# Attention loads in halves on a fixed SyncE order, turns in pairs, later memory rows and more gate matmuls in the memory attention's tail

## The chip, the cores and the metric

The kernel runs on one core of a Trainium2 chip. The metric is the device time of one execution in microseconds (us). The kernel before was timed in three runs: median 2069.23 us, from 2068.04 to 2072.08. One more execution was profiled; all rows of the profile and of the trace come from it.

## What is computed

The reference is a decoder trunk of two layers in float32 on x of 1024 tokens x 1024. Layer 0 mixes by dilated causal window attention in three groups of 8 heads, whose outputs are merged per head by their softmax denominators. Layer 1 mixes by a gated linear recurrence (HGRN2). Each layer also attends with 4 heads to 256 memory tokens and multiplies by a gate.

```python
for l in range(DEPTH):
    h = rms_norm(x, norm_gain[l])
    if l % 2 == 0:
        cols = h @ w_in_a[j]
        mix = dilated_mixer(cols[..., :3 * A_QKV], cos, sin, q_gain_a[j], k_gain_a[j])
        q_mem = cols[..., 3 * A_QKV:3 * A_QKV + MEM_WIDTH]
        gate = cols[..., 3 * A_QKV + MEM_WIDTH:]
...
    mem_out = memory_cross_attention(q_mem, mem, mem_norm_gain[l], w_mem_kv[l],
                                     mem_q_gain[l], mem_k_gain[l])
    y = jnp.concatenate([mix, mem_out], axis=-1) * jax.nn.silu(gate)
    x = x + y @ w_out
...
def dilated_mixer(cols, cos, sin, q_gain, k_gain):
...
    for g, (window, dil) in enumerate(DIL_PAIRS):
        o, lse = dilated_window_attention(q[:, :, g], k[:, :, g], v[:, :, g], dil, window // dil)
...
    alpha = jax.nn.softmax(jnp.stack(lses, axis=0), axis=0)
    o = jnp.sum(alpha[..., None] * jnp.stack(outs, axis=0), axis=0)
```

The groups are (128, 1), (512, 4) and (2048, 16): window and dilation. Head dimension is 128.

## The kernel before

**Engines and names.** TensorE (PE) multiplies and turns (transposes). ScalarE (ACT), VectorE (DVE) and GpSimd (POOL) work beside it, and SyncE (SP) issues nearly all DMAs, in the order of one queue: an issue that must wait holds back all that stand behind it. A product is made of three matmuls on a high and a low part of each side (wh, wl; hi, lo), which accumulate in a PSUM bank: tiles `acc` (three of them), `s` (two), `pt` (two, for turns) and `po` (one). ScalarE's copies (L174 and others) and VectorE empty them. The code is Python that is unrolled. Inside `with pinned()` every engine keeps the order in which the code is written; elsewhere a scheduler chooses. `with pinned(E.SP)` does that for SyncE alone.

**Projection of layer 0** (`step`, L1125). Column blocks of W_in are made as seven products each, with four steps per product. Step k issues 12 matmuls of 512 columns (`matmuls`, L1042 to L1044), then the spill of an older step's heads (`spill_heads`: a scaled copy by ScalarE, L1111, and a DMA to the DRAM buffer `qk_scr`), the emptying of the sums of step k - 1, the normalisation of step k - 3, and at its end `flip(k - BEHIND)`: four transposes (`heads_T`, L363) of the tile that was normalised, BEHIND = 6 steps late. Of the nine column groups six (q and k) are flipped, 16 tiles each, 96 flips in all.

**Memory rows** (loop at L1369). Eight steps without matmuls of their own end the projection (k = 1 to 8). In each, 12 matmuls of the generator `memory_steps` are issued: first the gate's columns for the memory part (L591), later the keys and values of the memory tokens. `mem_turn(0)` and `mem_turn(1)` turn the two blocks of normed memory rows: two tiles of four transposes each (`transposed_split`, L346), emptied by ScalarE (`s3hi`, L174) and VectorE (`s3lo`, L324). They stand at the start of k = 3 and of k = 4. The gate's Tanh (L519) is the first use of its function table there.

**Memory attention** (`for m in range(NT + 6)`, NT = 8). For m below 8 a block of 128 queries is projected (L1476 to L1478), normed, turned (`mem_query`, L363), scored against the memory's keys (`mem_scores`, L429 to L431), turned again (`mem_turned`, L458) and multiplied with the values (`mem_values`, L472 to L474), each a step or more behind the one ahead. From m = 8 on no queries are left, and between the two half steps stand gate matmuls of `cover` (`gate_mem_steps`, L591), as many as the table `under` says: 48 in all. Weights come as pieces (`load_piece`, DMA L204; `ahead` splits them into wh and wl on ScalarE and VectorE). At m = 8 head 0 of the attention is fetched whole.

**Attention over heads** (`for at, (g, hp) in enumerate(heads)`). Twelve pairs of heads, eight steps each: scores (L1537), masked and exponentiated by VectorE (L1540) and ScalarE (L1542), turned (L1551) two steps later, multiplied with the values two steps after that (L1564, `values`). Every second step one bank is full. For groups 1 and 2 `spill` copies it to one of three `os` tiles (L174) and writes it to `o_scr` by two DMAs (L1584). For group 0 `merge` (L1616) combines it with the other groups' rows, which come back by DMA as `og` (L1522) and are weighted by GpSimd (L1607), and writes by L1618. In the steps of group 2, the cheapest for TensorE, three gate matmuls more are issued, 96 in all. `fetch_qk` (L1394, L1396) loads kT and qT of the next head but one at m = 0, `fetch_v` (L1406, L1410, L1412) the values vv of the next head at m = 3; each is a DMA of 1 MB (two halves for group 1).

After it come the rest of the gate, the output projection (L662 to L664) and layer 1, which the change does not touch.

## Time and profile before

| | us |
|---|---|
| median of three runs | 2069.23 (2068.04 to 2072.08) |
| the profiled execution | 2065.92 |
| its span | 2064.0 |
| TensorE busy | 2030.8 (98%) |
| VectorE busy | 1276.9 (62%) |
| ScalarE busy | 889.1 (43%) |
| GpSimd busy | 570.8 (28%) |
| granted TensorE clock, mean over the span | 0.998 |

The span runs from the first to the last instruction; 1.9 us of the execution's time lie outside. Matmuls overlap, so that the start of one to the start of the next is what it costs, not its own duration (0.39 us for 512 columns, started every 0.23). In rows of waits, "PE po L1564 <- ACT os L174" reads: TensorE, at line 1564, on tile `po`, waited for ScalarE's instruction on `os` at line 174. PEld is the loading of the stationary side, which overlaps the matmuls. SPq is SyncE's queue of issues; the time of a row there is the issuing, and the landing of the data comes later.

### The profile page before, as it was taken

The page shows a single profiled execution, that of the slowest core. Times are in us where ns is not written, and L with a number is a line of the kernel's source. Part 1 is how long each engine was busy: PE and PEld are TensorE (multiplying, and loading weights), DVE is VectorE, ACT ScalarE, POOL GpSimd, SP SyncE. Part 2 cuts the span into 40 slices and gives each one's busy share as a digit, 9 for nine tenths or more (in the row PEclk, how much of TensorE's full clock was granted, in tenths as well). Part 3 has the DMA queues.
Part 4 walks back from the last instruction along what each step waited for, and adds up shares of the span by engine and source line. Part 5 has one row for each costly group of instructions (what it writes and reads, how often), then busy time and mean ns, then how long its engine had stood idle before and what let it go on. Part 6 is the DMA issues. An engine that isn't in the chain of part 4 may idle for free.

```text
span 2064.0 us, 29805 instructions
## 1 busy us (share of the span) xinstructions
PE 2030.8 (98%) x10641; PEld 1716.9 (83%) x10641; DVE 1276.9 (62%) x2540; ACT 889.1 (43%) x1678; POOL 570.8 (28%) x690
## 2 busy tenths in 40 slices
PE   7999999999999999999999999999999999999999
PEld 6888888888888887888898888877888888888887
DVE  7746866736767357555567454574554788876543
ACT  6435555633554345446666332253354323232220
POOL 4105765703755046131133200160031000000221
PEclk9999999999999999999999999999999999999999
DMA  6445999553544426527998474513354111213643
GB/s 228 133 133 103 95 142 132 108 168 90 120 119 134 152 72 195 172 70 264 313 333 265 153 250 153 170 61 132 125 173 142 32 51 45 79 42 102 236 133 112
DMA packets 431907, 295.59 MB, mean 143 GB/s; under 512 B 221568, under 2 KB 349840, under 8 KB 429712
## 3 DMA queue, kind: packets, MB, share of 16 engines
q1 hardware_dynamic: 418560, 276.91, 48.2%
q10 hardware_dynamic: 13200, 16.78, 2.2%
q8 instruction: 85, 1.39, 0.3%
q14 instruction: 62, 0.51, 0.1%
HBM read 202.28 MB, written 91.36 MB: 142 GB/s over the span
## 4 chain that ended last, share of the span: by engine, by line
PE 44%; DMA 4%; DVE 2%; ACT 2%; issue 1%; POOL 0%; SPq 0%; ACTq 0%; DVEq 0%
PE acc L662 4%; PE acc L663 4%; PE acc L664 4%; PE acc L558 4%; PE acc L556 4%; PE acc L557 4%; PE acc L1991 2%; DMA o_scr<-os 2%; PE s L2136 2%; PE pt L2136 2%; PE s L1537 1%; DMA og<-o_scr 1%; PE acc L1564 1%; PE po L1564 1%; PE pt L1551 1%; PE po L2270 1%
## 5 line engine op out<-in xcount | busy, mean ns | idle before, releaser
L174 ACT ACTIVATE wh<-raw 128x1024 fp32r<-128x1024 f32 x207 | 217.3, 1053 | 189.6 <-PE acc L557 60.0
L975 DVE TENSOR_TENSOR wl<-raw,wh 128x1024 fp32r<-128x1024 f32 x136 | 172.4, 1268 | 121.0 <-ACT wh L174 120.6
L1087 POOL TENSOR_TENSOR rr<-rv,nhalf 128x4 f32<-128x4 f32 x96 | 122.4, 1276 | 390.8 <-DVE rv L1085 390.2
L183 POOL TENSOR_TENSOR rr<-rv,nhalf 128x4 f32<-128x4 f32 (+1 forms) x46 | 43.1, 938 | 604.3 <-DVE rv L181 577.7
L662 PE MATMUL acc<-wh,yhi 128*128 128x512 f32 x360 | 142.7, 399 | 0.5 <-ACT yhi L174 0.5
L1042 PE MATMUL acc<-wh,hhi 128*128 128x512 f32 x360 | 141.9, 394 | 0.0
L663 PE MATMUL acc<-wl,yhi 128*128 128x512 f32 x360 | 141.1, 392 | 0.0
L1044 PE MATMUL acc<-wh,hlo 128*128 128x512 f32 x360 | 140.4, 390 | 0.0
L664 PE MATMUL acc<-wh,ylo 128*128 128x512 f32 x360 | 140.2, 394 | 0.0
L1043 PE MATMUL acc<-wl,hhi 128*128 128x512 f32 x360 | 140.2, 389 | 0.0
L556 PE MATMUL acc<-hhi,wh 128*128 128x512 f32 x320 | 128.7, 402 | 0.0
L557 PE MATMUL acc<-hlo,wh 128*128 128x512 f32 x320 | 127.6, 399 | 0.0
L558 PE MATMUL acc<-hhi,wl 128*128 128x512 f32 x320 | 127.4, 398 | 0.0
L236 DVE TENSOR_TENSOR wl<-raw,wh 128x1024 fp32r<-128x1024 f32 x62 | 76.6, 1239 | 66.4 <-ACT wh L174 60.8
L1542 ACT ACTIVATE pa<-pa,st 128x128 f32<-128x128 f32 (+1 forms) x192 | 84.5, 442 | 49.3 <-DVE st L1540 47.9
L979 DVE TENSOR_TENSOR raw<-raw 128x1024 f32<-128x1024 f32 x76 | 94.9, 1257 | 16.5 <-DMA raw<-in_w_in_a_dram 14.2
L674 DVE TENSOR_TENSOR x<-x,acc 128x512 f32<-128x512 f32 x62 | 42.1, 685 | 71.7 <-PE acc L664 71.7
L1540 DVE CUSTOM_DVE_ANT_0 pa<-s,masks 128x128 f32<-128x128 f32 (+1 forms) x192 | 59.6, 348 | 42.7 <-PE pt L1551 19.7
L1044 PEld LDWEIGHTS acc<-wh,hlo 128*128 128x128 f32 x360 | 67.6, 188 | 14.4
L1537 PE MATMUL s<-kT,qT 128*128 128x128 f32 (+1 forms) x384 | 78.2, 326 | 1.2 <-DVE st L1540 0.9
L662 PEld LDWEIGHTS acc<-wh,yhi 128*128 128x128 f32 x360 | 67.7, 188 | 14.0 <-ACT yhi L174 0.8
L664 PEld LDWEIGHTS acc<-wh,ylo 128*128 128x128 f32 x360 | 67.6, 188 | 13.9
(477 smaller groups left out, 5705.7 us busy)
## 6 DMA issues: line engine op xcount, KB each, us to landing
raw<-in_w_in_a_dram SPq DMA_DIRECT2D x109, 512.0 KB, 4.4
raw<-in_w_in_b_dram SPq DMA_DIRECT2D x43, 512.0 KB, 3.8
qk_scr<-m SPq DMA_DIRECT2D x48, 256.0 KB, 3.6
o_scr<-os SPq DMA_DIRECT2D x96, 128.0 KB, 5.8
kT<-qk_scr SPq DMA_DIRECT2D x8, 1024.0 KB, 6.3
qT<-qk_scr SPq DMA_DIRECT2D x8, 1024.0 KB, 9.0
vv<-v_scr SPq DMA_DIRECT2D x8, 1024.0 KB, 7.3
og<-o_scr SPq DMA_DIRECT2D x32, 256.0 KB, 5.5
```

Of the source, the lines that this page charges most:

```text
L174: A.activation(dst, src, AF.Copy)
L556: T.matmul(ps[:], wh[:, k, :], mh, start=k == 0, stop=False)
L557: T.matmul(ps[:], wh[:, k, :], ml, start=False, stop=False)
L558: T.matmul(ps[:], wl[:, k, :], mh, start=False, stop=k == 7)
L662: T.matmul(pss[ch][:], hi[:, k, :], wh[:, j, :], start=first and k == 0, stop=False)
L663: T.matmul(pss[ch][:], hi[:, k, :], wl[:, j, :], start=False, stop=False)
L664: T.matmul(pss[ch][:], lo[:, k, :], wh[:, j, :], start=False, stop=end and k == 3)
L975: V.tensor_tensor(lo[:], source(n, h), hi.bitcast(F32), op=OP.subtract)
L1042: T.matmul(flat, hi, wh, start=kt == 0 and p in (0, 1, 5), stop=False, **on)
L1043: T.matmul(flat, hi, wl, start=False, stop=False, **on)
L1044: T.matmul(flat, lo, wh, start=False, stop=kt == 3, **on)
L1087: G.tensor_tensor(r[:], sd[:], nhalf[:, :4], op=OP.pow)
```

## The change

It has five parts. The turns of the projection (**flips**) are made two at a time, in every second step, and both spills follow in the step behind. The turning of **memory rows** is put later: the first block after step k = 3, the second after four matmuls of k = 4; a Tanh on one column, whose result nobody reads, stands at k = 1. In the **tail** of the memory attention `under` holds 66 gate matmuls instead of 48, and weight pieces are loaded earlier and split at other steps. In the **attention** 78 gate matmuls are left for the 32 steps of group 2: two in each of the first 18 steps and three in each of the last 14, where there were three in each. And **loads** of kT, qT and vv are issued in halves of 512 KB, one per step (m = 0, 1, 2, 6 for kT and qT, m = 3, 4 for vv; head 0's six in six half steps of the tail), on a SyncE order that is fixed as written. TensorE has the same instructions as before, ScalarE one more, SyncE 24 more DMA issues.

```diff
@@ -1127,7 +1127,9 @@
             n, i = divmod(k, 4)
             if k <= LAST and k not in sums_at:
                 sums_at[k] = matmuls(k)
-            spill_heads(k - 1 - BEHIND)
+            if (k - BEHIND) % 2 == 0:
+                for t in (2, 1):
+                    spill_heads(k - t - BEHIND)
             if k - 1 in sums_at:
                 emptied(k - 1, sums_at.pop(k - 1))
             normed(k - 3)
@@ -1141,7 +1143,9 @@
             if fill:
                 fill()
             spread(k - 1)
-            flip(k - BEHIND)
+            if (k - BEHIND) % 2:
+                for t in (1, 0):
+                    flip(k - t - BEHIND)
 
         wraws, W, gates = {}, {}, {}
 
@@ -1368,11 +1372,15 @@
         ahead_of = memory_steps()
         for k in range(1, BEHIND + 3):
             with pinned():
-                if k in (3, 4):
-                    mts.append(mem_turn(k - 3))
-                for _ in range(96 // (BEHIND + 2)):
+                if k == 1:
+                    A.activation(small.tile([128, 1], F32, name="ss1")[:], nhalf[:, 0:1], AF.Tanh)
+                for j in range(96 // (BEHIND + 2)):
+                    if (k, j) == (4, 4):
+                        mts.append(mem_turn(1))
                     next(ahead_of)
                 step(LAST + k, lambda: pieces(LAST + k))
+                if k == 3:
+                    mts.append(mem_turn(0))
         sw.close()
 
         s1 = ExitStack()
@@ -1390,10 +1399,13 @@
             for i, t in ((1, k), (0, q)):
                 if g == 1:
                     src = qk_scr[i][g].rearrange("p h s -> p (h s)").rearrange("p (a h c) -> p a h c", a=2, c=512)
-                    for a in range(2):
-                        LQ.dma_start(t[:].rearrange("p h (a c) -> p a h c", a=2)[:, a], src[:, a, 2 * hp:2 * hp + 2])
-                else:
-                    LQ.dma_start(t[:], qk_scr[i][g][:, 2 * hp:2 * hp + 2])
+                    to = t[:].rearrange("p h (a c) -> p a h c", a=2)
+                for a in range(2):
+                    if g == 1:
+                        LQ.dma_start(to[:, a], src[:, a, 2 * hp:2 * hp + 2])
+                    else:
+                        LQ.dma_start(t[:, a], qk_scr[i][g][:, 2 * hp + a])
+                    yield
 
         def fetch_v(at):
             if at >= len(heads):
@@ -1402,23 +1414,19 @@
             pool = rooms_[at % 2]
             v = pool.tile([128, NT, 256], F32, name="vv", bufs=1)
             src = v_scr[g][:, hp * 256:(hp + 1) * 256]
-            if g == 0:
-                LQ.dma_start(v[:], src.rearrange("(m p) c -> p m c", p=128))
-            elif g == 1:
-                src = src.rearrange("(a p b) c -> p a b c", a=2, b=4)
-                for a in range(2):
-                    LQ.dma_start(v[:, 4 * a:4 * a + 4], src[:, a])
-            else:
-                LQ.dma_start(v[:], src.rearrange("(p m) c -> p m c", m=8))
             st = pool.tile([128, 128], F32, name="st", bufs=1)[:, 0:NG * NT * 4].rearrange("p (g m a h) -> p g m a h", g=NG, m=NT, a=2)
+            heads_at[g, hp] += v, st
+            src = src.rearrange(("(m p) c -> p m c", "(a p b) c -> p a b c", "(p m) c -> p m c")[g], **({"p": 128}, {"a": 2, "b": 4}, {"m": 8})[g])
+            for a in range(2):
+                LQ.dma_start(v[:, 4 * a:4 * a + 4], src[:, a] if g == 1 else src[:, 4 * a:4 * a + 4])
+                yield
             if g == 0:
                 for i in range(2):
                     LQ.dma_start(st[:, 1 + i].rearrange("p m a h -> p m (a h)"), st_scr[i, hp].rearrange("(m p) c -> p m c", p=128))
-            heads_at[g, hp] += v, st
 
         def fetch(at):
-            fetch_qk(at)
-            fetch_v(at)
+            yield from fetch_qk(at)
+            yield from fetch_v(at)
 
 
         with ExitStack() as sm:
@@ -1460,9 +1468,14 @@
             mprob, mattn = (sm.enter_context(tc.tile_pool(name=n, bufs=2, reuse_waits="tile")) for n in ("mprob", "mattn"))
             prob = lambda: mattn.tile([128, 2, MEM], F32, name="pm", bufs=6)[:]
             W = take("qmem_a", 4)
-            cover = gate_mem_steps(MG0[1])
+
+            def fillers():
+                for i in MG0[1:] + MG1:
+                    yield from gate_mem_steps(i, False)
+
+            cover, first_heads = fillers(), fetch(0)
             normed_, qs, shown, turned_ = {}, {}, {}, {}
-            under = {NT: (8, 8), NT + 1: (5, 5), NT + 2: (4, 4), NT + 3: (3, 3), NT + 4: (2, 2), NT + 5: (2, 2)}
+            under = {NT: (8, 8), NT + 1: (5, 5), NT + 2: (4, 4), NT + 3: (5, 5), NT + 4: (6, 6), NT + 5: (5, 5)}
             for m in range(NT + 6):
                 with pinned():
                     if m < NT:
@@ -1476,20 +1489,28 @@
                                 T.matmul(acc[:], hi[k], wh, start=k == 0, stop=False)
                                 T.matmul(acc[:], hi[k], wl, start=False, stop=False)
                                 T.matmul(acc[:], lo[k], wh, start=False, stop=k == 7)
-                                if m == NT - 1 and k % 2:
-                                    ahead(1 + k // 2)
+                                if m == NT - 1 and k in (1, 5):
+                                    ahead(1 + k // 4)
+                                    load_piece()
                         else:
                             for _ in range(under[m][h]):
                                 next(cover, None)
 
                     if m == 0:
                         later.pop(0)()
+                    if m == 5:
+                        load_piece()
+                        load_piece()
                     half_step(0)
                     if m == NT:
                         del W
-                        ahead(4)
+                        ahead(2)
+                        load_piece()
+                    if m == NT + 1:
+                        ahead(3)
+                    if m >= NT:
                         with pinned(E.SP):
-                            fetch(0)
+                            next(first_heads, None)
                     if m - 6 in turned_:
                         mem_values((m - 6) // 2, (m - 6) % 2, turned_.pop(m - 6), vm, om_scr)
                     if m - 5 in shown:
@@ -1497,14 +1518,15 @@
                     if later:
                         later.pop(0)()
                     half_step(1)
+                    if m >= NT:
+                        with pinned(E.SP):
+                            next(first_heads, None)
                     if m < NT:
                         normed_[m] = head_norm(acc[:], mattn, bufs=2)
                     if m - 1 in normed_:
                         qs[m - 1] = mem_query(normed_.pop(m - 1), mattn)
                     if 3 <= m < NT + 3:
                         shown[m - 3] = mem_scores((m - 3) // 2, (m - 3) % 2, qs, km, prob)
-            for _ in cover:
-                pass
 
         if True:
             ap_ = s1.enter_context(tc.tile_pool(name="attn", bufs=2, reuse_waits="tile"))
@@ -1618,20 +1640,21 @@
                     Y.dma_start(tile_of(o_scr[0][hp // 2], m + i)[:, hp % 2 * 256:hp % 2 * 256 + 256],
                                  y[:, 2 * i:2 * i + 2].rearrange("p h d -> p (h d)"))
 
-            def fillers():
-                for i in MG1:
-                    yield from gate_mem_steps(i, False)
-
-            fill = fillers()
+            fills = [48 * (1 + len(MG1)) - sum(map(sum, under.values())), 4 * NT]
             scored, turned, rest = [], [], []
-            fetch_qk(1)
+            for _ in fetch_qk(1):
+                pass
             for at, (g, hp) in enumerate(heads):
+                qk, vs_ = fetch_qk(at + 2), fetch_v(at + 1)
                 for m in range(NT):
-                    with pinned():
+                    with pinned(E.PE, E.SP):
                         new = (g, hp, m, *scores(g, hp, m))
                         old = turn_(*scored.pop(0)) if len(scored) > 1 else None
-                        for _ in range(3 if g == 2 else 0):
-                            next(fill, None)
+                        if g == 2:
+                            give = fills[0] // fills[1]
+                            fills[:] = fills[0] - give, fills[1] - 1
+                            for _ in range(give):
+                                next(cover)
                         if soon:
                             soon.pop()()
                         if len(turned) > 1:
@@ -1641,18 +1664,15 @@
                         before = scored[-1] if scored else None
                         if before and before[0] == 0 and before[2] % 2:
                             rest.append(weigh(before[1], before[2] - 1))
-                        if g == 1 and hp % 2:
+                        if g == 1 and hp != 2:
                             {0: load_piece, 6: lambda: split_piece(0), 7: lambda: split_piece(1)}.get(m, lambda: None)()
                         if g == 0 and m % 2:
                             others(hp, m - 1)
-                        if m == 0:
-                            fetch_qk(at + 2)
-                        if m == 3:
-                            fetch_v(at + 1)
+                        next(vs_ if 3 <= m < 6 else qk, None)
                     scored.append(new)
                     if old:
                         turned.append(old)
-            for _ in fill:
+            for _ in cover:
                 pass
 
             def last_turn():
```

The order of instructions shows it at three places. On ScalarE, at the memory rows, before (L1111 empties turned heads, s3hi are the turned memory rows, os is the gate's Tanh):

```order
L221 ACTIVATE wh<-raw,tabs 128x512 x2
L1111 ACTIVATE w_6746<-pt 128x512
L519 ACT_TABLE_LOAD
L519 ACTIVATE os<-acc 128x512
L1111 ACTIVATE w_6746<-pt 128x512
L174 ACTIVATE s3hi<-pt 128x512 x2
L1111 ACTIVATE u_6594<-pt 128x512
L174 ACTIVATE s3hi<-pt 128x512 x2
```

and the same place after:

```order
L221 ACTIVATE wh<-raw,tabs 128x512 x3
L519 ACTIVATE os<-acc 128x512
L1111 ACTIVATE w_6746<-pt 128x512 x2
L174 ACTIVATE s3hi<-pt 128x512 x4
L221 ACTIVATE wh<-raw,tabs 128x512 x2
L519 ACTIVATE os<-acc 128x512
L1111 ACTIVATE u_6594<-pt 128x512
L1111 ACTIVATE u_6619<-pt 128x512
```

The table load no longer stands ahead of the gate's Tanh and of L1111, two of the turned heads are emptied one after the other, and the four copies of memory rows stand together with no other copy between them.

On SyncE, in the tail of the memory attention, before (om_scr receives the memory attention's results, gatem_scr the gate's, raw are weight pieces; kT, qT, vv are head 0's):

```order
L477 DMA om_scr<-os 128x2x256
L204 DMA raw<-in_w_in_a_dram 128x2x512 x2
L1396 DMA kT<-qk_scr_97 128x2048
L1396 DMA qT<-qk_scr_94 128x2048
L1412 DMA vv<-v_scr_100 128x8x256
L204 DMA raw<-in_w_in_a_dram 128x2x512
L477 DMA om_scr<-os 128x2x256 x2
L595 DMA gatem_scr<-os 128x512
```

and after (the same loads, by lines 1407 and 1421 of the changed kernel):

```order
L204 DMA raw<-in_w_in_a_dram 128x2x512 x2
L1407 DMA kT<-qk_scr_97 128x1024
L477 DMA om_scr<-os 128x2x256
L1407 DMA kT<-qk_scr_97 128x1024
L1407 DMA qT<-qk_scr_94 128x1024
L477 DMA om_scr<-os 128x2x256
L595 DMA gatem_scr<-os 128x512
L1407 DMA qT<-qk_scr_94 128x1024
L1421 DMA vv<-v_scr_100 128x4x256
L477 DMA om_scr<-os 128x2x256
```

Three loads in a row have become halves with a result write after one or two of them, and no weight piece is loaded behind them.

On SyncE in the attention, around heads of group 1 whose results go to o_scr_106, and of group 2 with o_scr_104, before:

```order
L1406 DMA vv<-v_scr_98 128x8x256
L1575 DMA st_scr<-st 128x16
L1584 DMA o_scr_106<-os 128x256 x2
L1416 DMA st<-st_scr 128x8x4 x2
L1394 DMA kT<-qk_scr_96 128x2x512 x2
L1394 DMA qT<-qk_scr_93 128x2x512 x2
L1575 DMA st_scr<-st 128x16
L1584 DMA o_scr_104<-os 128x256 x6
```

and after:

```order
L1407 DMA kT<-qk_scr_97 128x1024
L1606 DMA o_scr_106<-os 128x256 x2
L1407 DMA kT<-qk_scr_97 128x1024
L1407 DMA qT<-qk_scr_94 128x1024
L1606 DMA o_scr_106<-os 128x256 x2
L1600 DMA st_scr<-st 128x32
L1421 DMA vv<-v_scr_98 128x4x256 x2
L1606 DMA o_scr_104<-os 128x256 x2
```

Before, six writes to o_scr of one head were issued in a row behind four loads; after, a pair of writes stands behind every one or two halves.

## The prediction

> **What bounds the kernel now.** I read the page first, then TensorE's waits over the two stages that the change touches, then the stretches of eight microseconds there, and last the timeline around each wait.
>
> The page's first part gives busy time, share of the span and instructions of each engine:
>
> ```profile
> PE 2030.8 (98%) x10641; PEld 1716.9 (83%) x10641; DVE 1276.9 (62%) x2540; ACT 889.1 (43%) x1678; POOL 570.8 (28%) x690
> ```
>
> TensorE is busy for 2030.8 of 2064.0 us, and the change removes none of its matmuls. So the change can only win some of the 33.2 us in which TensorE stands still, or time in which its matmuls run slowly. What TensorE waited for from 780 us to 965 us (end of the projection, memory rows, memory attention), as engine, tile and line, then total us, times and longest:
>
> ```profile
> PE pt L346 <- ACT w L1111: 1.6, 1, 1.6
> PE po L474 <- DVE pml L324: 1.5, 3, 0.9
> PE pt L363 <- DVE pml L324: 1.5, 1, 1.5
> PE po L472 <- ACT pmh L174: 0.7, 1, 0.7
> PE pt L346 <- ACT u L1111: 0.3, 1, 0.3
> ```
>
> The same from 965 to 1160 us, the attention over heads:
>
> ```profile
> PE po L1564 <- ACT os L174: 3.9, 2, 2.9
> PE po L1564 <- DVE os L1616: 1.3, 2, 1.0
> PE pt L1551 <- ACT pa L1542: 0.8, 2, 0.6
> PE s L1537 <- DVE st L1540: 0.2, 1, 0.2
> ```
>
> The first list holds 1.9 us at the memory rows (both L346 rows) and 1.5 + 1.5 + 0.7 = 3.7 us in the tail of the memory attention. The second holds 5.2 us at L1564, where a bank of results can't be emptied. The stretches (busy us of PE, PEld, DVE, ACT and POOL, granted clock, DMA share, GB/s) say why:
>
> ```profile
> 944.00:952.00 8.00, 6.97 (x47) 5.83 (x47) 2.68 (x8) 4.97 (x14) 2.04 (x2) 1.00 0.10 35
> 960.00:968.00 8.00, 8.00 (x58) 7.34 (x58) 4.15 (x25) 4.97 (x22) 0.00 (x0) 1.00 1.02 398
> 1024.00:1032.00 8.00, 6.19 (x35) 5.72 (x36) 3.59 (x18) 3.15 (x11) 2.73 (x3) 0.79 0.93 275
> 957.00:1112.00 155.00, 147.73 (x1066) 135.27 (x1066) 96.78 (x481) 104.31 (x389) 26.41 (x24) 0.99 0.99 329
> ```
>
> In the tail the DMA engines are nearly idle (share 0.10). In the attention, over 155 us, they are occupied throughout (0.99), at 329 GB/s on average, though 398 is reached: occupied, but not at their best rate. From 1024 us on the clock falls to 0.79, right behind the longest wait. The timeline there (start, duration; an idle time ahead of it in brackets):
>
> ```profile
> 1013.64 2.71 SPq L1394 DMA_DIRECT2D kT<-qk_scr  x2
> 1018.41 4.63 SPq L1584 DMA_DIRECT2D o_scr<-os  x6
> 1025.16 0.60 ACT L174 ACTIVATE os<-po 128x512 f32<-128x512 f32 x1 [0.62 <-DMA o_scr<-os]
> 1025.81 2.07 PE L1564 MATMUL po<-vv,pts 128*128 128x128 f32 x8 [2.94 <-ACT os L174]
> ```
>
> Loads go out in a burst ahead of result writes; the writes land late, `os` has no free buffer, ScalarE can't empty `po`, and TensorE waits 2.94 us.
>
> **Part by part. Turns in twos.** 96 turns of four transposes become 48 pairs. In the projection a turn of four and what follows it, and in the memory attention a turn of two tiles of four, look like this:
>
> ```profile
> 224.81 0.60 PE L363 MATMUL pt<-ident,w 128*128 128x128 f32 x4
> 225.16 0.48 PE L1042 MATMUL acc<-wh,hhi 128*128 128x512 f32 x1
> 225.48 0.40 PE L1043 MATMUL acc<-wl,hhi 128*128 128x512 f32 x1
> 225.71 0.40 PE L1044 MATMUL acc<-wh,hlo 128*128 128x512 f32 x1
> ...
> 895.54 1.03 PE L458 MATMUL pt<-ident,pm 128*128 128x128 f32 x8
> 896.33 0.47 PE L1476 MATMUL acc<-wh,hhi 128*128 128x512 f32 x1
> 896.64 0.39 PE L1477 MATMUL acc<-wl,hhi 128*128 128x512 f32 x1
> ```
>
> Starts count. Four transposes and the next matmul take 225.48 - 224.81 = 0.67 us, so two turns with two matmuls 1.34. Eight and one matmul take 896.64 - 895.54 = 1.10, with a second matmul (225.71 - 225.48 = 0.23) 1.33. A pair saves 0.01, 48 of them **0.5 us**. Were eight transposes as quick as two fours (2 x 0.35 = 0.70 for 0.79) it would be 0.10 a pair, 4.8 us: the other end. I take 0.5, since L458's eight fill two tiles as a pair of flips does. On the losing side a pair needs both `pt` tiles empty and brings two ScalarE copies (L1111) together; ScalarE at 43% and a whole second step hide that, and one late copy would cost 0.6 us (the 0.60 of the L174 row above, the same size).
>
> **Memory rows.** The timeline around both turns of memory rows:
>
> ```profile
> 803.63 1.28 ACT L519 ACT_TABLE_LOAD   x1
> 806.06 0.66 PE L346 MATMUL pt<-ident,raw 128*128 128x128 f32 x4 [1.58 <-ACT w L1111]
> 810.65 0.65 PE L346 MATMUL pt<-ident,raw 128*128 128x128 f32 x4 [0.31 <-ACT u L1111]
> ```
>
> The table load of 1.28 us stands ahead of the copy that empties `pt`. The dummy Tanh takes it to a place where no TensorE instruction waits for ScalarE; there it costs nothing (1.3 us if it hits a waiting copy). Turning later removes the wait for L1111: 1.9 us off. But the second turn now follows four gate matmuls (4 x 0.23 = 0.9 us) behind the first, and its tiles must be emptied by copies of 0.6 us each, so a new wait of 0 to 1.3 us arises; I take 0.5. Sum **-1.4**.
>
> **Tail.** Rows of the long waits:
>
> ```profile
> 920.10 1.06 ACT L174 ACTIVATE wh<-raw 128x1024 fp32r<-128x1024 f32 x1 [2.50 <-DMA raw<-in_w_in_a_dram]
> 928.33 0.66 PE L363 MATMUL pt<-ident,qn 128*128 128x128 f32 x4 [1.50 <-DVE pml L324]
> 938.38 0.60 ACT L519 ACTIVATE os<-acc 128x512 f32<-128x512 f32 x1 [3.26 <-DMA om_scr<-os]
> ```
>
> ScalarE stood 2.50 us for a weight piece, and all behind it came late, which TensorE pays 8 us later; loaded at m = 5 and m = 7 that piece is there. The other waits, those at L474 and L472 in the list, fall where two or three fillers lie between dependent steps; now five or six do. Eighteen matmuls move here from the attention: 18 x 0.23 = 4.1 us, enough for 3.7 us of waits. I leave 0.5 for the row at 938.38 (gate results waiting for `os` behind a write), which more gate work can repeat. Sum **-3.2**: tail +0.9, attention -4.1. If the waits lie elsewhere than the fillers, 0; if all go, -3.7.
>
> **Attention.** Without 18 matmuls and with halves spread over steps, the o_scr writes go between halves. Of the 5.2 us at L1564 I leave 1.0 for the queues that stay busy: -4.2 (ends 0 and -5.2). The dip goes with its wait: 8 x (1 - 0.79) = -1.7 (ends 0 and -1.7). Against it, 18 g=2 steps have two fillers where they had three:
>
> ```profile
> 962.44 0.61 PE L1537 MATMUL s<-kT,qT 128*128 128x128 f32 x4
> 964.25 0.61 PE L1537 MATMUL s<-kT,qT 128*128 128x128 f32 x4
> L1542 ACT ACTIVATE pa<-pa,st 128x128 f32<-128x128 f32 x104 | 40.7, 393 | 28.8 <-DVE st L1540 27.4 <-issue 1.1
> L1542 ACT ACTIVATION_READ_ACCUMULATOR pa<-pa,st 128x1 f32 x192 | 36.1, 188 | 0.0
> ```
>
> A step takes TensorE 1.81 us, then 1.58; ScalarE needs 2 x (0.393 + 0.188) + 0.60 / 2 = 1.46. ScalarE is near enough to make some steps late: +1.5 (ends 0 and all 4.1). Sum **-4.4**.
>
> The Trainium skill ("TensorE: Matmul & The Clock Gate", Part 1) says that the clock halves after an idle window of about 3.4 us. The trace shows it lower behind 2.94 us; if the rule held and the dip had another cause, its 1.7 would stay and the sum be 1.7 smaller.
>
> Total: -0.5 - 1.4 - 3.2 - 4.4 = **-9.5 us**. The profiled execution took 2065.92, 3.3 below the median of 2069.23: its own time would become 2056.4. On the median that is **2059.7 us**.
>
> **The rivals.**
>
> *Writes still wait.* A half still lies ahead of a write, so 5.2 and 1.7 us stay: -9.5 + 4.2 + 1.7 = -3.6, 2065.6. For it: `os` has three buffers as before. Against: one half, not a burst, stands there.
>
> *The transfers set the attention.* Share 0.99: then its length stays, the removed matmuls and waits return as waits for loads, and the tail gets 0.9 longer: -0.5 - 1.4 + 0.9 = -1.0, 2068.2. Against: TensorE waits for no kT, qT or vv in the list above, and head 0's loads move into the empty tail.
>
> *ScalarE sets the thinned steps*: 4.1 instead of 1.5 comes back, -6.9, 2062.3.
>
> *Slower: SP's fixed order.* SP's waits from 918 us to 1160 us, and two kinds of load:
>
> ```profile
> SPq L1522 <- POOL og L1607: 18.2, 9, 3.9
> kT<-qk_scr SPq DMA_DIRECT2D x8, 1024.0 KB, 6.3
> kT<-qk_scr SPq DMA_DIRECT2D x8, 512.0 KB, 5.3
> o_scr<-os SPq DMA_DIRECT2D x96, 128.0 KB, 5.8
> og<-o_scr SPq DMA_DIRECT2D x32, 256.0 KB, 5.5
> ```
>
> Where an `og` load waits for GpSimd, the write behind it waits too, for `os`, then ScalarE and TensorE. The last half of a `qT`, issued at m = 6, is needed ten steps of 1.6 us later, so it decides only from a stand of some 9 us. The writes decide sooner: three `os` buffers last 3 x 2 steps of 1.6 us, 9.6, and a write takes 5.8 to land, so from a stand of 3.8 us. If half of the 18.2 us reaches TensorE while nothing of 5.9 us is won: -9.5 + 5.9 + 9.1 = +5.5, 2074.7. Against: the longest of the nine waits is 3.9 us, their mean 2.0.
>
> *Slower: halves cost queue time.* Doubling kT adds only 1.0 us to 5.3, so 4.3 of a half's 5.3, about 0.8, doesn't shrink with size. Now 24 whole loads are cut; with 96 writes, 32 `og` loads and 24 halves (kT, qT and vv 8 each) there were 176 issues, and become 200. If the fixed part fills the engines, the stage grows by 24 / 176 x 0.8 x 155 = 17 us: -1.0 + 17 = +16, 2085. Against: the stretch from 960 us moves 398 GB/s with halves of group 1 in it, so transfers overlap.
> The Trainium skill ("DMA: Bandwidth & Descriptors", Bandwidth) asks for 1 MiB or more a transfer for 75% of peak; its fixed 2.0 us ("Anatomy of one DMA") times 24 would be an estimate of 48 us if nothing overlapped. By that rule too it would be slower.
>
> **How the numbers follow.** Forecast 0.52, writes still wait 0.12, transfers 0.12, ScalarE 0.14, SP's order 0.07, halves' cost 0.03. With 0.2% (4.1 us, about what a measurement of this kernel can tell from no change) the border is 2065.1. Faster: 0.50 of the forecast, 0.13 of ScalarE, 0.04 of the writes: 0.67. Slower: both last and 0.01 of transfers: 0.11. Within: 0.22. The forecast's own bounds: best without the far end of the turns -0.5 - 1.9 - 3.7 - 6.9 = -13.0, 2056.2, and a part of that far end takes it to 2054.5. Upward the range reaches to the transfers' 2068.2; the slower rivals and the far end of the turns stay out.
>
> **What would show it.** Right: no row for L346 above 0.6 us; the rows at L363, L474 and L472 under 1 us together; L1564's waits near 1.0 us, the clock at 1.00 from 957 to 1112 us, no burst of six o_scr issues. Wrong: new waits of L1537 for kT or qT (transfers), of L1551 for `pa` or of L1537 for `st` beyond 3 us (ScalarE), long SP waits for `og` with L1564 behind them (SP's order), landings of halves near those of wholes with waits for them (halves). If the sum of TensorE's waits falls by 8 us and the time doesn't, the forecast fails as a whole.

## The result and the profile after

The changed kernel takes 2058.61 us (median of four runs, 2054.53 to 2060.97) where the kernel before takes 2069.55: the ratio is 0.9946, 95% interval [0.9931, 0.9961]. Five more runs later gave 0.9944 [0.9931, 0.9958]. That is 11 us, 0.54% faster, against a forecast of 9.5. One execution of the kernel with turns only, below, took 10878.59 us and is in no mean.

One profiled execution alone shows less, since single executions scatter: 74 later runs of the kernel before have a mean of 2068.8 us and a standard deviation of 2, and its first profile, with 2065.92, was among its shorter ones, while the changed kernel's first, with 2060.63, was among its longer ones. So stages are compared below over all profiles, and times over all runs.

The first part of the page after:

```profile
PE 2027.8 (98%) x10641; PEld 1718.6 (83%) x10641; DVE 1275.4 (62%) x2540; ACT 884.2 (43%) x1679; POOL 571.0 (28%) x690
```

The work is the same. TensorE's waits from 780 to 965 us:

```profile
PE pt L363 <- DVE pml L324: 1.3, 1, 1.3
PE acc L389 <- DVE qn L357: 0.8, 1, 0.8
PE po L474 <- DVE pml L324: 0.5, 1, 0.5
PE pt L346 <- DVE s3lo L324: 0.4, 1, 0.4
PE acc L389 <- DVE wl L233: 0.3, 1, 0.3
```

and in the attention (L1559 is the scores, L1573 the turns, L1586 the products with vv):

```profile
PE po L1586 <- DVE os L1638: 3.2, 4, 1.4
PE s L1559 <- DVE st L1562: 2.0, 5, 0.9
PE pt L1573 <- ACT pa L1564: 1.3, 4, 0.5
```

In the attention TensorE waits 6.5 us, as long as before (6.4). But the waits are many and short, the longest 1.4 us where it was 2.94 (2.3 us in the second profile). The stretches that answer to those of before:

```profile
944.00:952.00 8.00, 8.00 (x50) 7.09 (x49) 4.56 (x7) 4.80 (x10) 1.75 (x2) 1.00 0.34 116
960.00:968.00 8.00, 8.00 (x68) 7.76 (x67) 4.70 (x29) 6.17 (x26) 0.00 (x0) 1.00 1.03 372
1024.00:1032.00 8.00, 8.00 (x61) 7.33 (x60) 6.19 (x32) 3.22 (x14) 5.51 (x6) 1.00 0.98 331
957.00:1112.00 155.00, 150.72 (x1107) 138.26 (x1106) 101.94 (x503) 109.00 (x408) 26.48 (x24) 1.00 1.00 330
```

TensorE is busy throughout the tail stretch (8.00 for 6.97), the clock stays at 1.00, and the DMA engines are as occupied as before (1.00, 330 GB/s): the same bytes, in halves and in another order.

Where the time lies is best seen by stages, cut at starts in the trace: the projection (from its first matmul at L1042 to its last one on `hhi`, at 783.54 us before; the four groups on `s4hi` behind that one count with the next stage), the memory rows (to the first qn turn), the memory attention (to the first scores), the attention with what follows it (to the first matmul of the output projection), and the rest to the end of the last matmul. All profiles of this study, in us:

| kernel | projection | memory rows | memory attention | attention | rest |
|---|---|---|---|---|---|
| before | 715.40 | 57.22 | 113.88 | 234.15 | 871.37 |
| before, again | 715.38 | 57.42 | 112.73 | 236.79 | 870.11 |
| changed | 712.52 | 57.78 | 115.01 | 228.27 | 872.40 |
| changed, again | 712.52 | 58.60 | 114.92 | 227.85 | 870.17 |
| turns only | 712.52 | 60.51 | 112.26 | 235.42 | 872.54 |
| rows only | 715.41 | 57.33 | 113.04 | 234.59 | 870.09 |
| turns and rows | 712.52 | 58.44 | 112.31 | 237.56 | 871.95 |
| turns and rows, again | 712.52 | 57.67 | 112.44 | 235.00 | 871.94 |
| tail only | 715.40 | 57.30 | 114.87 | 234.12 | 872.97 |
| halves only | 715.38 | 57.10 | 113.32 | 234.44 | 872.80 |
| all but the tail | 712.53 | 59.08 | 112.45 | 231.42 | 871.57 |
| all, order free | 712.52 | 57.73 | 115.44 | 231.31 | 869.45 |
| all, whole loads | 712.53 | 57.78 | 114.40 | 232.20 | 872.42 |
| all, three og | 712.53 | 57.95 | 115.19 | 225.55 | 871.11 |

The projection repeats to 0.03 us; the rest, which nothing here touches, scatters from 869.5 to 873.0. The attention nearly adds up. Over the stage, TensorE's idle time and what the lower clock takes (half of each stretch at 0.50) come to 11.2 us in the mean of the six profiles with before's loads and fillers, and to 7.3 in the two of the changed kernel. These 3.9 us and the 4.1 of the 18 matmuls moved away make 8.0; the stage is 7.5 us shorter (228.06 for 235.6). For the first pair of profiles alone it closes less well: 4.1, the dip's 1.7 and 0.7 of waits make 6.5, and the stage is 5.9 us shorter.

### The profile page after: what moved, and what is told of

It reads as the page before. It is cut to its first block, busy times and chain, and to the rows that moved or that the text cites. A ratio compares the mean times of both kernels' runs of the same rounds, so it can differ in the third digit from the quotient of the medians.

```text
span 2058.8 us, 29797 instructions
## 1 busy us (share of the span) xinstructions
PE 2027.8 (98%) x10641; PEld 1718.6 (83%) x10641; DVE 1275.4 (62%) x2540; ACT 884.2 (43%) x1679; POOL 571.0 (28%) x690
## 4 chain that ended last, share of the span: by engine, by line
PE 44%; DMA 3%; DVE 2%; ACT 1%; POOL 1%; issue 1%; SPq 0%; DVEq 0%; ACTq 0%; POOLq 0%
PE acc L662 4%; PE acc L663 4%; PE acc L664 4%; PE acc L558 4%; PE acc L556 4%; PE acc L557 4%; PE acc L2011 2%; PE s L2156 2%; PE pt L2156 2%; PE s L1559 1%; PE acc L292 1%; PE acc L293 1%; PE acc L294 1%; DMA og<-o_scr 1%; PE po L1586 1%; PE po L2290 1%
## 5 line engine op out<-in xcount | busy, mean ns | idle before, releaser
L1042 PE MATMUL acc<-wh,hhi 128*128 128x512 f32 x360 | 141.3, 393 | 0.0
L1559 PE MATMUL s<-kT,qT 128*128 128x128 f32 (+1 forms) x384 | 77.6, 325 | 2.0 <-DVE st L1562 2.0
```

Source lines behind the costliest of these rows:

```text
L1042: T.matmul(flat, hi, wh, start=kt == 0 and p in (0, 1, 5), stop=False, **on)
```

## The experiments

**Each part alone.** Four kernels made from the one before. Turns only:

```diff
-            flip(k - BEHIND)
+            if (k - BEHIND) % 2:
+                for t in (1, 0):
+                    flip(k - t - BEHIND)
```

(with the spills as in the change).

> The kernel before with the turns of the projection in pairs and nothing else. Theory (a pair of turns costs what L458's eight transposes cost): 0.5 us faster, 2069.0. Rival (eight transposes cost twice a lone four's 0.35, or a whole switch to the next matmul is saved): up to 4.8 us faster, 2064.8. In the traces the first turn of memory rows (L346) stands at 758.9 us before and at 757.3 in the changed kernel; if the 1.6 us between them come from the turns, this run has it near 757.3 too.

Ratio 0.9987 [0.9976, 0.9997], 2.7 us by it. The projection is 2.88 us shorter in this profile and in every one with pairs. (The row at 758.9 and 757.3 us in the expectation is a turn at L1315, not at L346, which first stands at 803.88 us before; here the L1315 turn starts at 757.15 us, so that sign came true.) But the memory rows got 3.2 us longer:

```profile
803.21 1.28 ACT L519 ACT_TABLE_LOAD   x1
804.99 1.08 ACT L1111 ACTIVATE w<-pt 128x512 f32<-128x512 f32 x2
805.64 1.82 PE L346 MATMUL pt<-ident,raw 128*128 128x128 f32 x8 [3.60 <-ACT w L1111]
808.11 0.63 PE L591 MATMUL acc<-hhi,wl 128*128 128x512 f32 x1
809.56 0.39 PE L591 MATMUL acc<-hhi,wh 128*128 128x512 f32 x1
```

Both `pt` tiles are now full when the table load begins, so the wait at L346 grows from 1.58 to 3.60 us, and behind it matmuls take 0.63 us instead of 0.39: the granted clock is 0.57 over the next four microseconds. The prediction had named this cover (ScalarE's second step) but not that the table load falls into it.

Rows only (the diff's parts at `mem_turn` and Tanh):

```diff
+                if k == 1:
+                    A.activation(small.tile([128, 1], F32, name="ss1")[:], nhalf[:, 0:1], AF.Tanh)
```

> The kernel before with the memory rows turned later and the early Tanh. Theory of the prediction: 1.4 us faster, the two waits at L346 (1.6 and 0.3) replaced by one of about 0.5. Rival, from the trace of the changed kernel: nothing gained, since new waits at L346 (s3lo, 0.4) and at L389 (acc, 0.8 and 0.3) take the place of 1.9; time the same as before.

Ratio 0.9988 [0.998, 0.9997]. The stage itself gained nothing, 57.33 us for 57.22 and 57.42. TensorE's waits from 780 to 850 us:

```profile
PE acc L389 <- DVE qn L357: 0.9, 1, 0.9
PE pt L346 <- ACT u L1111: 0.3, 1, 0.3
```

The wait of 1.6 us is gone, and a wait for a normed key (L389) has come, as the rival said. From what other stage the 2.5 us of the runs come, this profile doesn't show; the intervals of this run and of turns only both end just short of no change.

Tail only (fillers 66 and 78, pieces earlier, loads as before):

```diff
-            under = {NT: (8, 8), NT + 1: (5, 5), NT + 2: (4, 4), NT + 3: (3, 3), NT + 4: (2, 2), NT + 5: (2, 2)}
+            under = {NT: (8, 8), NT + 1: (5, 5), NT + 2: (4, 4), NT + 3: (5, 5), NT + 4: (6, 6), NT + 5: (5, 5)}
```

> The kernel before with 66 gate matmuls in the memory attention's tail, 78 in the attention and the weight pieces loaded earlier; kT, qT and vv whole and on SyncE's old order. Theory: the tail waits of 3.7 us fall to about 0.5, and the attention is shortened by 4.1 us of matmuls less 1.5 that ScalarE and VectorE give back; the 5.2 us at L1564 and the clock's dip stay: 1.7 us faster, 2067.8. Rival (transfers set the attention): the attention gives back all 4.1, the time stays 0.9 us above or at before's, and the waits at L1564 grow beyond 8 us.

Ratio 1.0001 [0.9992, 1.0009]: nothing, as the rival has it. In the tail the waits at L472 and L474 are gone. The attention with whole loads gave back what it was spared (234.12 us for 234.15 and 236.79); its waits:

```profile
PE po L1575 <- DVE os L1627: 4.3, 1, 4.3
PE po L1575 <- ACT os L174: 2.9, 2, 2.6
PE s L1548 <- DVE st L1551: 2.1, 2, 1.9
```

Halves only (fillers 48 and 96):

```diff
-                    with pinned():
+                    with pinned(E.PE, E.SP):
...
-                        if m == 0:
-                            fetch_qk(at + 2)
-                        if m == 3:
-                            fetch_v(at + 1)
+                        next(vs_ if 3 <= m < 6 else qk, None)
```

> The kernel before with kT, qT and vv in halves on SyncE's written order, fillers 48 and 96 as before. Theory (bursts of loads ahead of the writes cause the waits at L1564): those fall from 5.2 to about 1.0 and the dip of the clock near 1024 us goes, 5.9 us faster, 2063.6. Rival (the halves only work with fewer fillers, or halves cost queue time): L1564 still waits 4 us or more, within 2 us of before, or slower.

(`pinned()` without names keeps the written order on TensorE alone, not on every engine as said above; so SyncE's order in the attention was free before, and this edit fixes it.)

Ratio 0.9975 [0.9967, 0.9984], 5.2 us. TensorE has no wait at the products with vv any more, and no dip near 1024 us. The profiled execution is the slowest of its eleven, 2066.83 us, and its attention of 234.44 us is no shorter than before's: it shows that those waits went, not the 5.2 us. One other long wait stands in it:

```profile
1098.17 1.06 ACT L174 ACTIVATE wh<-raw 128x1024 fp32r<-128x1024 f32 x1 [4.83 <-DMA raw<-in_w_in_a_dram]
1099.77 1.18 PE L1554 MATMUL pt<-ident,pa 128*128 128x128 f32 x4 [3.69 <-ACT pa L1545]
```

A weight piece for the next gate columns landed late; ScalarE stood at its split for 4.83 us, with the exponentials behind it; TensorE waited 3.69 us, and the clock stood at 0.50 for two windows of 3.41 us. In the changed kernel pieces are loaded at three heads of group 1 instead of two and earlier in the tail, and no such row appears there, nor in the other kernels with halves and that edit. So the halves need that small edit beside them.

**Parts together.** Four more, on one chip with 16 runs of the kernel before:

> The changed kernel once more, for its time on the same chip as the three beside it and for a second profile. If the sum of the parts holds, about 10.5 us faster than before (turns 2.5, rows 3.2, tail 0, halves 5.4 by the means of the earlier runs give 10.7). If the parts help one another (turns need the early Tanh, the tail's fillers need the halves), more: 12 to 13.

Ratio 0.9944 [0.9931, 0.9958], mean 2057.3. The total is near the sum of the parts (11.9 us off a mean of 2069.3; 10.7 by the parts), but the next two runs show that the parts don't add up one by one.

> The changed kernel with fillers 48 and 96 as before, the weight pieces loaded where they were (turns, rows and halves kept). Theory: with the halves the attention gives the 18 matmuls back in full, so that this is 2 to 4 us slower than the changed kernel, although the same tail edit alone gained nothing. Rival (ScalarE or the loads set the thinned steps with halves too): within 1 us of the changed kernel.

(The edit: the parts of the diff at `under`, `fills` and the pieces are left out.) Ratio 0.997 [0.9959, 0.9982], mean 2062.6: 5 us slower than the changed kernel. The same tail edit that gains nothing on whole loads gains 5 with halves; by stages the attention is 3.4 us longer (231.42 for 228.06, the mean of the two) and the memory attention 2.5 shorter, which is 0.9 of the 5. The edit also puts the weight pieces back, and ScalarE stands for two of them in the attention, 4.2 us together. So the 5 us belong to fillers and pieces together, and no run parts them.

> The kernel before with the turns in pairs and the memory rows later with the early Tanh, attention untouched. Theory: turns alone paid 3.6 us at L346 and a clock dip behind it, which the early Tanh and the later rows take away; so together more than the sum of both alone (2.5 + 3.2): 6 to 7 us faster than before. Rival (both win the same waits, or what they win is lost again at L389 where weights and norms come late): 3 us or less.

Ratio 0.9971 [0.9962, 0.998] and, in eight more runs, 0.9977 [0.9967, 0.9987]: 5 to 6 us. The stage of memory rows is 58.4 and 57.7 us where turns alone made it 60.5; so the later turning and the early Tanh do pay together, but only for what the pairs would break. Projection and memory rows together: 2.88 off, about 0.9 back (mean of eight profiles with both, 58.1, against 57.3 for five without pairs), 2.0 us. The memory attention is shorter too in all four profiles with pairs and before's tail, 112.3 to 112.5 us for 112.7 to 113.9 in the four without pairs; why, they don't show.

> The changed kernel with the halves but SyncE's order in the attention left to the scheduler, which puts two kT and two qT halves together again. Theory (bursts ahead of the writes are what cost): the waits at L1586 for ScalarE's os come back, 3 us or more together, and 3 to 5 us of the gain are lost. Rival (size of a transfer is what counts): as quick as the changed kernel. Second rival (the fixed order costs by its stands for og): quicker than the changed kernel, waits on DVE os L1638 under 1 us.

```diff
-                    with pinned(E.PE, E.SP):
+                    with pinned():
```

Ratio 0.996 [0.9948, 0.9973], mean 2060.3, 3 us slower than the changed kernel beside it (its runs are 2058.74 to 2061.5, the changed kernel's 2054.75 to 2058.88; the two intervals overlap a little). The waits of before are back:

```profile
PE po L1586 <- ACT os L174: 4.7, 2, 2.6
PE po L1586 <- DVE os L1638: 2.6, 2, 2.0
```

Halves that go out two at a time, with four writes behind them, hold the writes back as whole loads did.

**Size, order and buffers.**

> The changed kernel with whole loads of 1 MB for groups 0 and 2 on the same fixed order: kT at m = 0, qT at m = 2, vv at m = 3. Theory (a burst ahead of the writes costs, not the size alone): between the changed kernel (2057.3) and the one whose order is left free (2060.3), 1 to 2 us slower than the changed kernel. Rival (size alone decides, each write waits for a whole load): 3 us or more slower. Second rival (halves cost queue time): faster than the changed kernel.

```diff
-                    else:
-                        LQ.dma_start(t[:, a], qk_scr[i][g][:, 2 * hp + a])
+                    elif a == 0:
+                        LQ.dma_start(t[:], qk_scr[i][g][:, 2 * hp:2 * hp + 2])
```

(and the same for vv). Ratio 0.9976 [0.9965, 0.9987], mean 2064.0: 6 to 7 us slower than halves, clear of the changed kernel's interval. That is more than the theory expected. Size matters in itself, in the way the rival said:

```profile
1097.74 0.44 SPq L1424 DMA_DIRECT2D vv<-v_scr  x1
1098.28 3.64 SPq L1609 DMA_DIRECT2D o_scr<-os  x2
1104.24 0.60 ACT L174 ACTIVATE os<-acc 128x512 f32<-128x512 f32 x1 [4.06 <-DMA o_scr<-os]
1105.08 1.10 PE L1562 MATMUL s<-kT,qT 128*128 128x256 f32 x4 [2.24 <-DVE st L1565]
```

Behind the whole vv the two writes of a bank take 3.64 us to issue, ScalarE waits 4.06 us for a free `os`, and the scores 2.24 us.

> The changed kernel with three buffers instead of two for the og tile that is kept until the merge (and three instead of four for pa, to make room). Theory: SyncE's stands of up to 7.4 us ahead of og loads come from that buffer; they shrink below 3 us, L1586 waits less than 1 us for DVE os L1638 instead of 3.2, and the time falls 2 to 3 us below the changed kernel's 2057.3. Rival (GpSimd's chain of 3.3 us per pair sets it): stands and time as in the changed kernel.

```diff
-                    o = ap_.tile([128, 2, 256], F32, name=f"og{g}")
+                    o = ap_.tile([128, 2, 256], F32, name=f"og{g}", bufs=4 - g)
```

(and three buffers for `pa`; only group 1's `og` gets the third). Ratio 0.9943 [0.9931, 0.9954], mean 2056.6: the same as the changed kernel. SyncE's stands in the changed kernel, and here:

```profile
SPq L1544 <- DVE os L1638: 22.2, 7, 7.4
SPq L1640 <- DVE os L1638: 14.1, 5, 4.6
```

```profile
SPq L1640 <- DVE os L1638: 24.1, 12, 11.3
SPq L1544 <- POOL og L1629: 13.8, 5, 6.2
```

The stands for the buffer went and stands for GpSimd's weighted sum came: the rival. TensorE's wait for DVE os is 3.1 us, as before that edit. The attention is the shortest of all (225.55), but the runs don't show it, and one profile doesn't settle 2 us.

> The kernel before once more, for a second profile. The first one took 2065.92 us, some 3 us less than this kernel's usual run. Theory: the 3 us lie where a transfer is waited for, in the attention (954.6 to 1188.8 us in the first profile, 234.2 us long), which is then 235 to 238 us here; projection and memory rows are the same to 0.3 us. Rival: they lie in layer 1 (871.4 us in the first).

The second profile of the kernel before has an attention of 236.79 us, in the range named; its projection repeats to 0.02 us.

> Turns in pairs and memory rows later once more, for a second profile: the first took 2067.07 us, the slowest of its runs (mean 2062.9). Theory: the gain of turns and rows is 2.8 us at the first scores (951.9 against 954.6 us), as in the first profile, and the rest of the 6.4 us that the runs give comes from an attention that lost 237.6 us in the first profile and usually less, about 233 to 235. Rival: the gain repeats as 1.4 us or less at the first scores, and the attention is as long as before's: then the time is 2065 to 2067 and the 6.4 was chance.

Mean 2063.4. At the first scores this kernel, at 950.55 us, is 4 us ahead of before (954.64 and 954.50; 951.85 in the first profile), and the attention takes 235.0. Up to 1 us of that is where the projection begins (67.92 us here, 68.14 and 68.97 before). Counted from there, the three stages up to the first scores are 3.1 us shorter in the mean of the two profiles. So turns and rows are worth more than 2.0 us, and the chance rival falls; but of 5 to 6 us the stages show about 3.

## Why the prediction came out right, point by point

**The mechanism.** TensorE had only waits and slow clock to lose, and lost them where the prediction put them: bursts of loads ahead of writes. The wait at the products with vv for ScalarE's `os`, 3.9 us before and 3.8 in its second profile, stands in neither profile of the changed kernel. Halves only shows it (those waits gone), and so does the free order (back again). That halves and the moved matmuls are one change and not two is what the prediction had as a rival and the forecast had not: with whole loads the attention gave back the matmuls (ratio 1.0001); with halves they and the earlier weight pieces are worth 5 us.

**Turns: mis-sized.** Forecast 0.5 us, measured 2.7. The stage is 2.88 us shorter, alike to 0.03 us in nine profiles, but 85 single turns stand in it before and 42 pairs, 84 turns, after: one turn moved past its end. A turn costs 3.203 - 12 x 0.227 = 0.48 us; the other 2.40 are 0.057 a pair, 2.7 us for 48. The rows of the changed kernel:

```profile
224.91 1.03 PE L363 MATMUL pt<-ident,w 128*128 128x128 f32 x8
225.70 0.48 PE L1042 MATMUL acc<-wh,hhi 128*128 128x512 f32 x1
226.02 0.40 PE L1043 MATMUL acc<-wl,hhi 128*128 128x512 f32 x1
...
231.25 1.04 PE L363 MATMUL pt<-ident,w 128*128 128x128 f32 x8
```

Up to the second matmul the pair costs what was worked out (226.02 - 224.91 = 1.11 for 1.10). But from one pair to the next lie 231.25 - 224.91 = 6.34 us, and two single turns with their matmuls take 2 x (228.02 - 224.81) = 6.42. The failing step is where I stopped counting: each turn makes the matmuls after it start a little later than 0.228 us apart, well past the second. The mean of 82 steps with 12 matmuls before (3.203 us) and of 35 pairs with 24 after (6.345) gives the same, 0.06 us a pair. A cost per switch is read from a whole period, not from the rows next to it.

**Memory rows: the sign.** Forecast 1.4 us won; the stage is 0.9 us longer with pairs, of which 0.5 is the turn that moved into it, and no shorter without. The step that failed is "turning later removes the wait": it did (L346 from 1.9 to 0.4 us), but weights and normed keys were next in line at L389 (0.29 and 0.76), which the prediction had no row for. With the turns the sum of both terms is 2.0 by stages for 1.9 forecast: two errors that cancel, which is luck.

**Tail: near.** The memory attention got 2.2 us longer (mean 115.0 of six profiles for 112.8 of eight) where 0.9 was forecast: of 3.7 us of waits about 1.9 went, for 3.2. One step failed: "loaded at m = 5 and m = 7 that piece is there". It wasn't:

```profile
918.36 1.06 ACT L174 ACTIVATE wh<-raw 128x1024 fp32r<-128x1024 f32 x1 [2.32 <-DMA raw<-in_w_in_a_dram]
926.58 0.66 PE L363 MATMUL pt<-ident,qn 128*128 128x128 f32 x4 [1.32 <-DVE pml L324]
```

ScalarE stood 2.32 us for 2.50 and TensorE 1.32 for 1.50. The waits between short fillers, at L472 and L474, fell from 2.2 to 0.5 us as forecast. Together with the row at L363 that is 1.8 us, where the prediction's sign of being right was under 1. The prediction's list of waits left out 0.7 us at the first scores (L1537); they went too.

**Attention: right in sum.** Forecast 4.4 beside the 4.1 of moved matmuls, 8.5; measured 7.5 (228.06 for 235.6, the mean of six profiles with before's loads and fillers). The dip went as forecast in one profile of two; in the second one stands behind a wait of 2.29 us, and the stage is no longer for it (227.85). The waits at L1586 fell to 3.2 us, not 1.0, and those at L1559 and L1573 rose by 2.3, not 1.5: ScalarE's rival was there, in part. SyncE's order does stand ahead of the `og` loads, up to 7.4 us, past the 3.8 us from which that rival decides. But with a third `og` buffer these stands went and 3.1 us of waits at L1586 stayed, so it isn't shown that the stands cause them; and the free order costs 3 us more than the fixed one. A half of kT lands in 6.2 us, a whole one in 6.3 before: the sign that the prediction named for the rival of queue time. But no wait for kT, qT or vv came with it, o_scr writes land in 5.5 us for 5.8, and whole loads on the same order are 6 to 7 us slower. The Trainium skill ("DMA: Bandwidth & Descriptors", Bandwidth) asks for 1 MiB or more, from a table of loads that GpSimd issues, and the fixed 2.0 us that the prediction takes from it ("Anatomy of one DMA") is of that path too; these loads are SyncE's, and here the trace and that rule differ. The rate is no lower, 330 GB/s for 329, and what counts here is who waits behind.

**What stays open.** By runs, turns and rows together win 5 to 6 us, and halves on top of them without the tail's fillers less than 1 (0.997 for 0.9971), though halves alone win 5.2. So both win partly the same microseconds. The stages don't show which: profiles of kernels that are alike there differ by up to 3.4 us in the attention and 3.5 in the rest. Nor is it shown where rows alone win 2.5 us. And the two profiled executions of the changed kernel are 7.0 us shorter than the two of before, not 11: the stages account for those 7, and where the runs find the other 4, no profile shows.

## What to carry to other kernels

Where one queue carries bulk loads and small results, cut and spread the loads before anything is moved out of that stage: with bursts in place, taking 4 us of matmuls away won nothing; with halves, the same edit won 5. Of a switch between kinds of work, measure the whole period. And when a wait is taken away, look for the row that is next in line and for what the edit beside it puts into its cover.

## What the runs showed of the hardware

The clock dips behind idle time, and what counts is not the single wait but a fixed grid of windows. In fourteen profiles all changes of the granted clock after the first 20 us lie on a grid of 3.413 us, whose start differs from run to run, and each dip is one window of it at 0.50 (once two). Cut into these windows between 40 and 2040 us, TensorE's idle time decides in every case: behind all 22 windows with 1.90 us or more of it a dip follows, and none begins behind a window with less (the nearest has 1.895). By single waits the edge is blurred: from 740 to 1190 us the mean granted clock of the four microseconds behind a wait was 0.50 to 0.64 for all eleven from 2.44 us up, 0.57 to 0.68 for three of seven from 1.91 to 2.29 us, and 1.00 for all eighteen from 1.4 to 1.9 us. Rows only has both kinds, a wait of 1.91 us that brought a dip and one of 2.21 us that didn't. Their windows (busy us of PE comes first, the clock is third from the end):

```profile
999.80:1003.21 3.41, 1.29 (x10) 0.90 (x10) 1.76 (x14) 1.83 (x8) 0.00 (x0) 1.00 0.92 272
1003.21:1006.62 3.41, 3.41 (x15) 2.94 (x14) 1.20 (x6) 1.96 (x9) 0.00 (x0) 0.50 1.00 357
1023.69:1027.10 3.41, 1.61 (x11) 1.22 (x9) 0.78 (x4) 2.79 (x11) 3.41 (x5) 1.00 1.04 333
1027.10:1030.51 3.41, 3.01 (x23) 2.86 (x24) 2.25 (x12) 1.01 (x3) 2.05 (x2) 1.00 0.88 214
```

The shorter wait shares its window with other idle time, 2.12 us in all; the longer one is cut by the grid into 1.8 and 0.4 us. A dip takes 1.71 us of TensorE's clock (half of 3.41). The Trainium skill's rule ("TensorE: Matmul & The Clock Gate", Part 1) has an idle window of about 3.4 us; the trace agrees with the window's length, but 1.9 us of idle time in it were enough here. So many short waits are cheaper than one long one of the same sum, as long as they don't meet in one window.

In three kernels TensorE also stood still for 1.6 to 2.1 us in the attention with nothing in the profile that released it ("issue"):

```profile
PE s L1548 <- issue: 2.1, 1, 2.1
```

(all but the tail). What it waited for is not shown.
